# One PSUM tile of six banks in place of several pools, and eight attention columns kept in SBUF

## The chip, the core and the metric

The kernel runs on one core of a Trainium2 chip. The metric is the device time of one execution in microseconds (us); the kernel before takes 2475.04 us, the median of three runs (2474.16 to 2475.89). Five engines run side by side, each taking its own instructions in order: PE (matrix products), PEld (the loading of PE's stationary operand), DVE and ACT (element-wise work), POOL (element-wise work, little used here), and the queues that issue DMAs, of which SP's carries nearly all loads. PE can write its products only into PSUM, a memory of eight banks of 512 float32 values per partition, from which DVE or ACT copies or adds them into SBUF. This copying is called an eviction below.

## The reference

One layer of a decoder that mixes three branches, for a prompt of 1024 tokens and eight sample tokens (TT = 1032 columns in all), width 1024:

```python
xn = rmsnorm(x)
sc_b, sc_c, sc_x, z, xbc, dt_raw, q, gates = split(xn @ w_in)
y_a = (sc_b * conv3(sc_c * sc_x)) @ w_sc_out                  # short convolution
xs, bm, cm = split(silu(conv4(xbc) + b))                      # Mamba-2 SSD, 32 heads x 64, state 128
y_b = group_rmsnorm((ssd(xs, dt, bm, cm) + d * xs) * silu(z)) @ w_ssm_out
y_c = softmax(q @ mem_k.T / 16) @ mem_v @ w_attn_o            # 4 heads x 256, 256 memory tokens
x += (g_a * y_a + g_b * y_b + g_c * y_c) @ w_merge_o          # g = sigmoid(gates)
x += (silu(rmsnorm(x) @ w_gate) * (rmsnorm(x) @ w_up)) @ w_down
y = rmsnorm(x)
```

The sample tokens have key and value caches of their own, so their attention is computed apart from the prompt's. Beside y the new states of the convolutions and of the SSD and the memory's keys and values are returned.

## The kernel before

Activations lie transposed in SBUF: 128 rows of the model width by 1032 columns of tokens, eight such tiles for the width. Every float32 operand of a large product is split into a high and a low part (`split_act` and `st_split`: an ACT copy for the high part, a DVE subtraction for the low one), and a product is three products of these parts.

There are two kinds of large product. A **plain product** (`gemm`, L200) makes one block of 128 output rows by 1032 columns in a buffer of three banks from `mm_ps` (L67): the pool `pmm` has two such buffers, taken in turn, so that one can be evicted while the next is filled. A **Strassen pair** (`strassen`, L311) makes two neighbouring blocks of output rows at once from seven half-size products, in the order B11, T1, nT2, B21, T3, B22, T4. Each has 24 rows of two matmuls (L266) into a buffer of two banks from `st_ps` (L257). There are three such buffers, `m0`, `m1` and `m2`, each a tile of its own, in the pools `pst1` and `pst`: B11, nT2, T3 and T4 go into the first (`pa`), each but B11 added onto what stands there, T1 and B22 into the second (`pb`), B21 into the third (`pc`). After a product its buffer is read at once into the quarter of the result that needs it: B11, T1 and nT2 by ACT (L321), or by DVE where the result is added into x (`into`, L319), B21, T3 and B22 by DVE (L380, L395, L398), and T4 by whoever called. Which of the three buffers plays which part alternates from one Strassen pair to the next (`tags`), with a special order for the first two.

Six banks serve the large products, and the two left (`psm`, L70) the small ones: transposes, scores, the SSD's states. The six are given out by pools that are closed and opened again where the kernel passes from plain products to Strassen pairs or back.

In order of time:

- to about 130 us: x is loaded, normed and transposed; the products dt and B0 (`ps_dt`, `ps_B0`), then C0, z0 and z1 as plain products; the first Strassen pair (Z2).
- 130 to 957: the other 39 Strassen pairs of the input projection (X, Z, G, C, B), with the convolutions on DVE.
- 957 to 1585: the SSD's scan and the attention in small matmuls, among them as plain products the queries (`ps_q`, evicted at L806), four gates (L816), and the 24 output products of the two first branches (`po`, L1440, L1444, L1447).
- 1585 to 1680: the attention's output (`po3`, L1729), eight plain products.
- 1680 to 1770: the merge (`pm`, L1800, evicted at L1807) in halves of 516 columns, in 16 buffers.
- 1770 to 2215: gate and up of the FFN, 22 Strassen pairs. Six of them (`early`) have their products B11 and B21 made ahead in `st_early` (L272) together.
- 2215 to 2473: eight Strassen pairs of the down projection, added into x by DVE; from 2378 on eight plain products (`pd`, L2000) and a last part (`pl`, L2052 to L2062) with three products in one buffer of three banks, each bank evicted by an instruction of its own; the last norm and the stores.

The order on each engine is worked out ahead, when the program is made, from the order in which the kernel states the instructions and from modelled durations. Waits between engines follow from which instructions read and write a tile.

The attention's result for the prompt is written to `at_d` in DRAM by column block, and the eight sample columns, computed into `o_s` (64 columns of the constant tile `tri`), by a DMA of their own in `s_back` (L1610). `out_load` (L1398) loads a tile of `at_d`, all 1032 columns, with one DMA on SP's queue as input of the attention's output product; two of these eight loads are put ahead of it by `out_ahead`.

Of the kernel before, what the change touches and what calls it, by code (L numbers as in the profile page):

```python
# [9 lines left out]
F32 = mybir.dt.float32  # L10
# [4 lines left out]
PSUM = bass.MemoryType.PSUM  # L15
DRAM = bass.MemoryType.DRAM

P = 128
D = 1024
T = 1024  # L20
NS = 8
TT = T + NS
NCH = 3
# [24 lines left out]
def tile_kernel(ctx: ExitStack, tc, a, o):  # L48
    nc = tc.nc
    V, S, G, PE, SY = nc.vector, nc.scalar, nc.gpsimd, nc.tensor, nc.sync  # L50
# [10 lines left out]
    ev = ctx.enter_context(tc.tile_pool(name="ev", bufs=5))  # L61
    dp = ctx.enter_context(tc.tile_pool(name="scratch", bufs=1, space=DRAM))
    psm = ctx.enter_context(tc.tile_pool(name="psm", bufs=2, space=PSUM))
    mm_stack = ExitStack()
    pmm = [mm_stack.enter_context(tc.tile_pool(name="pmm", bufs=2, space=PSUM))]

    def mm_ps(name):  # L67
        return pmm[0].tile([P, NCH, 512], F32, tag="mm", name=name)

    def sm_ps(name):  # L70
        return psm.tile([P, 512], F32, tag="sm", name=name)
# [24 lines left out]
    tri = cp.tile([P, P], F32, tag="tri", name="tri")  # L96
# [87 lines left out]
    def tick():  # L184
        if pend:
            f = pend.popleft()
            if f is not None:
                f()
# [42 lines left out]


    HS = [slice(0, HT), slice(HT, TT)]
    pst = [None]
    freed = [None]
    count = [0]

# [3 lines left out]
    def st_raw(src, name):  # L241
        raw = wp.tile([P, 1024], F32, tag="raw", name=name)
        if len(src.shape) == 4:
            for t in range(2):
                in_turn("raw", SY.dma_start(raw[:, t * 512 : (t + 1) * 512].rearrange("p (k c) -> p k c", k=4), src[:, t]))
            return raw
        in_turn("raw", SY.dma_start(raw.rearrange("p (k c) -> p k c", k=KD), src))
        return raw

    def st_split(src, name, n=1024):  # L250
        hi = wp.tile([P, 1024], F32R, tag="whi", name=name + "h")
        lo = wp.tile([P, 1024], F32R, tag="wlo", name=name + "l")
        in_turn("hi", S.copy(hi[:, :n], src))
        in_turn("lo", V.tensor_sub(lo[:, :n], src, f32(hi)[:, :n]))
        return hi, lo

    def st_ps(tag, name):  # L257
        return pst[0].tile([P, 2, 512], F32, tag=tag, name=name)

    def st_prod(forms, ps, w, off, f, start):  # L260
        for kt in range(4):
# [49 lines left out]
    def strassen(  # L311
        src1, src2, forms, nm, sums, outs, early=None, after_t3=None, ready=None, hook=None, into=False,
        refill=None, following=None,
    ):


        def first(dst, ps):
            if into:
                V.tensor_tensor(dst, ps, dst, op=ALU.add)  # L319
            else:  # L320
                S.copy(dst, ps)  # L321

        def used(f):
            turning.append(refill(f) if refill is not None else None)
            if len(turning) > LATE:
                g = turning.popleft()
                if g is not None:
                    g()


        lead = ahead.pop() if ahead else None
        if lead is not None:
            raw1, raw2 = lead[0], st_raw(src2, f"{nm}r2")
        elif ready is None and early is None:
            raw1, raw2 = st_raw(src1, f"{nm}r1"), st_raw(src2, f"{nm}r2")
        if count[0] == 0:
            tags = ("m2", "m1", "m0")
        elif count[0] == 1:
            tags = ("m1", "m2", "m0")
        else:  # L340
            tags = ("m0", "m1", "m2") if count[0] % 2 == 0 else ("m2", "m1", "m0")
        count[0] += 1
        pa, pb = (st_ps(t, f"{nm}{t}") for t in tags[:2])

        def prod(ps, w, off, f, start):
            st_prod(forms, ps, w, off, f, start)

        o11, o12, o21, o22 = outs()
        if early is None:
            pc = st_ps(tags[2], f"{nm}{tags[2]}")  # L350
            wA = st_split(raw1, f"{nm}A") if lead is None else lead[1]
            prod(pa, wA, 0, "B11", True)
        else:
            tick()
        if ready is not None:
            raw1, raw2, sa, wS, wT = ready
        elif early is not None:
            raw1, raw2, sa, wS = st_sums(src1, src2, nm, sums, freed[0])
        else:
            sa = sums(f"{nm}sa")  # L360
            V.tensor_add(sa[:, :512], raw2[:, :512], raw2[:, 512:])
            V.tensor_add(sa[:, 512:], sa[:, :512], raw1[:, :512])
            wS = st_split(sa, f"{nm}S")
            first(o11, hv(pa))
            used("B11")
        if ready is None:
            sb = st_adds2(raw1, raw2, sa, nm, sums)
        if early is None:
            tick()
        if hook is not None:  # L370
            hook()
        prod(pb, wS, 0, "T1", True)
        first(o22, hv(pb))
        used("T1")
        prod(pa, wS, 512, "nT2", early is not None)
        if early is None:
            first(o12, hv(pa))
            used("nT2")
            prod(pc, wA, 512, "B21", True)
            V.tensor_tensor(o11, hv(pc), o11, op=ALU.add)  # L380
            used("B21")
        else:
            S.copy(o21, o12)
            V.tensor_sub(o22, o22, o12)
            freed[0] = V.tensor_tensor(o12, hv(pa), o12, op=ALU.add).ins
        if ready is None:
            wT = st_split(sb, f"{nm}T")
        if following is not None:
            raw = st_raw(following, f"{nm}f")
            wD = st_split(raw2[:, 512:], f"{nm}D", 512)  # L390
        tick()
        prod(pa, wT, 0, "T3", False)
        if after_t3 is not None:
            after_t3()
        V.tensor_tensor(o22, o22, hv(pa), op=ALU.subtract)  # L395
        used("T3")
        prod(pb, wT, 512, "B22", False)
        V.tensor_tensor(o12, o12, hv(pb), op=ALU.subtract)  # L398
        used("B22")
        tick()  # L400
        if following is None:
            wD = st_split(raw2[:, 512:], f"{nm}D", 512)
        else:
            ahead.append((raw, st_split(raw, f"{nm}F")))
        prod(pa, wD, 0, "T4", False)
        used("T4")
        if into:
            V.tensor_tensor(o21, o21, hv(pa), op=ALU.subtract)
            return
        if early is not None:  # L410
            V.tensor_tensor(o21, hv(pa), o21, op=ALU.add)
            return o21
        return hv(pa)
# [9 lines left out]
    at_d = dram("at_d", [8, P, TT])  # L423
# [17 lines left out]
    qs_d = dram("qs_d", [NS, D])  # L441
    os_d = dram("os_d", [NS, D])

    tail_sc = cp.tile([P, 1, 10, 8], F32, tag="tail_sc", name="tail_sc")
    tail_xc = cp.tile([P, 3, 11, 8], F32, tag="tail_xc", name="tail_xc")
    qs = cp.tile([P, 8, NS], F32, tag="qs", name="qs")
# [11 lines left out]
    h_xc = ch.tile([P, 24, 24], F32, tag="h_xc", name="h_xc")  # L458
    xn = [(act_tile("ah", f"xnh{k}"), act_tile("al", f"xnl{k}")) for k in range(KD)]
    xw = [act_tile(("ah", "al")[k % 2], f"xw{k}", F32) for k in range(KD)]  # L460
    ps_dt, ps_b0 = mm_ps("ps_dt"), mm_ps("ps_B0")

    with tc.tile_pool(name="p0", bufs=1) as p0:
        xin = []
# [12 lines left out]
        for key, src, n in (  # L477
# [14 lines left out]
            while done < n:  # L492
                b, off = divmod(at, P)
# [117 lines left out]
    for src, dst, nr, nt in (  # L611
# [4 lines left out]
        for q0 in range(0, nt, per):  # L616
            t = ev_tile(f"hist{nr}_{q0}", (nr, per * P))
# [710 lines left out]
        for kt in range(4):  # L1328
            split_to(*xforms["T3"][kt], raw3[kt // 2][:, HS[kt % 2]])

    mm_stack.close()
    mm_stack = ExitStack()
    st_stack = ExitStack()
    pst[0] = st_stack.enter_context(tc.tile_pool(name="pst1", bufs=1, space=PSUM))
    for i in (2, 4, 6, 8, 10, 12):
        z_pair(i, plain3 if i == 2 else None)
    flush()
# [38 lines left out]
            split_to(*xforms["T3"][kt], b12s[kt // 2][:, HS[kt % 2]])  # L1376

    gate_pair(18, plain)
    st_stack.close()
    pa_stack.close()  # L1380
    ch_stack.close()
    pmm[0] = mm_stack.enter_context(tc.tile_pool(name="pmm1", bufs=2, space=PSUM))

# [11 lines left out]

    def out_load(src, k):  # L1398
        t = ev_tile(f"in0{k}")
        SY.dma_start(t[:, :TT], src[k])  # L1400
        ahead.append(t)

    def out_in(src):
# [96 lines left out]
    if True:  # L1500
# [1 line left out]
        kTl = at.tile([P, KD, MEM], F32R, tag="kTl", bufs=1, name="kTl")  # L1502
        vh = at.tile([P, 2, D], F32R, tag="vh", bufs=1, name="vh")
        vl = at.tile([P, 2, D], F32R, tag="vl", bufs=1, name="vl")
        o_s = tri[:, :64].rearrange("p (t b) -> p t b", t=8)
        sc_s = tri[:, 64:].rearrange("p (m b h) -> p m b h", m=2, b=NS)
        pTs = qs.rearrange("p t b -> p (t b)").rearrange("p (m c) -> p m c", m=2)

# [94 lines left out]
        def s_back():  # L1603
            t = ev_tile("osr", (NS, D))
            SY.dma_start(t, os_d)
            ps = sm_ps("psob")
            for i in range(8):
                PE.transpose(ps[:, i * NS : (i + 1) * NS], t[:, i * P : (i + 1) * P], ident[:NS, :NS])
            V.tensor_copy(o_s.rearrange("p t b -> p (t b)"), ps[:, :64])
            SY.dma_start(at_d[:, :, T:TT].rearrange("t p b -> p t b"), o_s)  # L1610

        heads = {}
        slot = [None]
# [173 lines left out]
    for half in range(2):  # L1787
        sq = ev_tile(f"sq{half}")
        for m in range(KD):
# [16 lines left out]
            t = x2[m][:, HS[half]]  # L1806
# [12 lines left out]
            flush()  # L1819
            norm_half(1, sq)  # L1820
    aux_stack.close()
    mm_stack.close()

    st_stack = ExitStack()
    pst[0] = st_stack.enter_context(tc.tile_pool(name="pst", bufs=1, space=PSUM))
    pfx = st_stack.enter_context(tc.tile_pool(name="fx", bufs=2))
    fx["T4"] = lambda part, nm: pair_of(pfx.tile([P, AW], F32R, tag=part, name=nm))  # L1830

# [131 lines left out]
                into=True, hook=opening if ch == 0 and m == 0 else None, **turn,  # L1963
            )
    st_stack.close()
    pmm[0] = ctx.enter_context(tc.tile_pool(name="pmm2", bufs=2, space=PSUM))
    fin = ctx.enter_context(tc.tile_pool(name="fin", bufs=1))

    def hidden(j):
# [129 lines left out]
```

## Time and profile before

| | |
|---|---|
| median of three runs | 2475.04 us |
| profiled execution, its own time | 2474.8 us |
| its span (first to last instruction) | 2472.7 us |
| granted TensorE clock, mean | 0.994 |
| PE busy | 2428.5 us (98%) |
| PEld, DVE, ACT, POOL busy | 93%, 64%, 43%, 5% |
| chain that ended last | PE 86%, DMA 5%, DVE 5%, ACT 2% |

By stretch, in us (PE's and DVE's busy time):

| stretch | length | PE | DVE |
|---|---|---|---|
| 0 to 60 | 60 | 50.5 | 38.8 |
| 60 to 130 | 70 | 65.7 | 57.0 |
| 130 to 957, Strassen pairs | 827 | 824.5 | 558.8 |
| 957 to 1585, SSD and attention | 628 | 615.6 | 372.7 |
| 1585 to 1770, attention output and merge | 185 | 183.7 | 106.5 |
| 1770 to 2215, gate and up | 445 | 444.8 | 282.9 |
| 2215 to 2380, down | 165 | 160.3 | 117.4 |
| 2380 to 2473, end | 93 | 83.4 | 50.2 |

A row of the timeline reads: start in us, duration in us, engine, line, operation, the tile written and the tiles read (buffer numbers left out), shape, how many instructions the row joins, and in brackets how long the engine sat idle before it and what ended that. A row joining several matmuls lasts from the first one's start to the last one's end, and since matmuls overlap in PE, rows overlap too. A row of the waits reads: who waited for what, the us in total, how many times, and the longest. In a table by stretch, the stretch and its length come first, then the busy time with the number of instructions in brackets for each engine, then the granted clock, the DMA's busy share and GB/s. In the table of groups the count is followed by the busy time in us and the mean of one in ns, and then by the idle time ahead of them and its enders.

### The profile page before, as it was taken

What the parts mean: (1) busy time and instruction counts of PE and PEld (TensorE: products, weight loads), DVE (VectorE), ACT (ScalarE), POOL (GpSimd) and SP (SyncE); (2) the same over time, 40 slices, a digit from 0 to 9 for tenths busy, and PEclk for the clock granted to TensorE, in tenths of its full rate; (3) what the DMA queues carried; (4) which work ended last, traced back from release to release, by engine and by line L of the source; (5) the groups of instructions that cost most, each with busy time, mean ns of one, the idle gap of its engine ahead of it and who ended that gap; (6) DMA issues with size and microseconds to landing.
All of it is one profiled execution on the core that took longest, in us unless ns stands there. A gap on an engine that the chain in (4) does not pass through costs nothing.

```text
span 2472.7 us, 45688 instructions
## 1 busy us (share of the span) xinstructions
PE 2428.5 (98%) x18946; PEld 2310.5 (93%) x18946; DVE 1584.3 (64%) x2601; ACT 1067.1 (43%) x1712; POOL 114.8 (5%) x163
## 2 busy tenths in 40 slices
PE   8999999999999999999999999999999999999998
PEld 6899999999999999888888888899999999999998
DVE  6844586777677774666767562454787555476755
ACT  6654455354545535556545441223453333342322
POOL 0100000000000000121120000000000000000000
PEclk8999999999999999999999999999999999999999
DMA  6344434344344456667878677874454323264421
GB/s 195 121 139 154 132 102 153 112 130 131 108 137 137 129 154 210 194 207 254 265 219 286 205 265 238 266 241 153 141 174 134 108 86 112 74 231 132 156 85 69
DMA packets 359662, 404.42 MB, mean 164 GB/s; under 512 B 17446, under 2 KB 286870, under 8 KB 359447
## 3 DMA queue, kind: packets, MB, share of 16 engines
q1 hardware_dynamic: 339006, 343.79, 44.6%
q10 hardware_dynamic: 20449, 57.71, 6.0%
q8 instruction: 149, 2.44, 0.4%
q14 instruction: 58, 0.48, 0.1%
HBM read 286.35 MB, written 115.32 MB: 162 GB/s over the span
## 4 chain that ended last, share of the span: by engine, by line
PE 86%; DMA 5%; DVE 5%; ACT 2%; issue 1%; SPq 0%; ACTq 0%; POOL 0%; DVEq 0%
PE po L220 12%; PE ps_q L220 4%; PE pm L1800 3%; PE ps_g L220 2%; PE pd L220 1%; PE py L1041 1%; PE pss L1054 1%; PE po L1033 1%; PE Z2m L266 1%; PE Z4m L266 1%; PE X8m L266 1%; PE d12m L266 1%; PE C2m L266 1%; PE C4m L266 1%; PE G18m L266 1%
## 5 line engine op out<-in xcount | busy, mean ns | idle before, releaser
L986 ACT ACTIVATE r<-r,acum 128x128 f32<-128x128 f32 x256 | 79.2, 392 | 5.1 <-DMA r<-ac_d 4.7
L757 DVE SCALAR_TENSOR_TENSOR ax<-u,prm,ax 128x1024 f32<-128x1024 f32 x44 | 56.3, 1279 | 0.0
L927 ACT ACTIVATE st<-st,es 128x128 f32<-128x128 f32 x128 | 41.5, 392 | 26.4 <-DMA st<-in_state_ssm_dram 23.9
L1018 POOL TENSOR_TENSOR xdd<-xdt,decst 128x512 f32<-128x512 f32 x32 | 37.1, 1160 | 292.2 <-DVE xdt L1014 292.2
L1447 DVE TENSOR_TENSOR yr<-po,yr 128x1032 f32<-128x1032 f32 x8 | 9.8, 1230 | 55.1 <-PE po L220 45.2
L1037 DVE TENSOR_TENSOR y<-po,ea 128x512 f32<-128x512 f32 x28 | 19.3, 690 | 38.9 <-PE po L1033 38.9
L1012 DVE TENSOR_TENSOR r<-r,cbm 128x1024 f32<-128x1024 f32 x32 | 39.2, 1224 | 2.5
L929 DVE SCALAR_TENSOR_TENSOR st<-sr,dts,st 128x128 f32<-128x128 f32 x128 | 40.3, 345 | 0.4
L1011 ACT COPY bT<-bp 128x128 f32<-128x128 f32 x32 | 8.5, 265 | 64.3 <-DVE cbm L1009 64.2
L2034 ACT ACTIVATE fj<-psy 128x512 f32<-128x512 f32 (+1 forms) x18 | 10.7, 596 | 59.1 <-PE psy L2032 59.0
L933 DVE SCALAR_TENSOR_TENSOR sr<-st,sr 128x128 f32<-128x128 f32 x128 | 35.2, 285 | 1.1
L1054 PE MATMUL pss<-xdd,bT 128*128 128x512 f32 x64 | 33.4, 604 | 2.3 <-ACT bT L1011 2.3
L1041 PE MATMUL py<-r,xdt 128*64 128x128 f32 x512 | 35.0, 279 | 0.0
L987 ACT ACTIVATE r<-r 128x1024 f32<-128x1024 f32 x32 | 33.9, 1058 | 0.7
L1014 DVE TENSOR_TENSOR xdt<-xp,dtT 128x512 f32<-128x512 f32 x32 | 21.9, 684 | 18.7 <-PE xp L1007 18.5
L1807 DVE TENSOR_TENSOR x<-pm,xT 128x516 f32<-128x516 f32 x16 | 11.1, 695 | 35.1 <-PE pm L1800 35.1
L1067 POOL TENSOR_TENSOR s<-s,cdec 128x512 f32<-128x512 f32 x28 | 32.1, 1145 | 4.5 <-DVE s L1060 3.9
L1041 PEld LDWEIGHTS py<-r,xdt 128*64 128x64 f32 x512 | 27.3, 136 | 4.2 <-issue 0.5
L1033 PE MATMUL po<-bc,s 128*128 128x128 f32 x224 | 29.6, 275 | 0.0
L760 DVE SCALAR_TENSOR_TENSOR ax<-u,prm,ax 128x1032 f32<-128x1032 f32 x22 | 28.3, 1286 | 0.0
L1178 DVE SCALAR_TENSOR_TENSOR x<-x,prm,sqa 128x1032 f32<-128x1032 f32 x16 | 19.7, 1288 | 13.3 <-ACT sqa L1174 13.3
L1033 PEld LDWEIGHTS po<-bc,s 128*128 128x128 f32 x224 | 27.7, 191 | 0.5
(9066 smaller groups left out, 9044.0 us busy)
## 6 DMA issues: line engine op xcount, KB each, us to landing
r<-ac_d SPq DMA_DIRECT2D x32, 512.0 KB
gt<-gt_d SPq DMA_DIRECT2D x24, 516.0 KB
xs_d<-ax ACTq DMA_DIRECT2D x22, 516.0 KB
gt_d<-G ACTq DMA_DIRECT2D x20, 516.0 KB
x<-xs_d SPq DMA_DIRECT2D x16, 516.0 KB
zs<-zs_d SPq DMA_DIRECT2D x16, 516.0 KB
yb_d<-x SPq DMA_DIRECT2D x16, 516.0 KB
in<-yb_d SPq DMA_DIRECT2D x16, 516.0 KB
```

The lines of the kernel that those rows point to most:

```text
L220: PE.matmul(out[:, c : c + n], wt[:, ks], x[:, c : c + n], start=(k == 0 and i == 0), stop=(k == nk - 1 and i == 2),)
L266: PE.matmul(hv(ps)[:, c : c + n], wt[:, ks], x[:, c : c + n], start=(start and kt == 0 and i == 0), stop=(kt == 3 and i == 2), skip_group_ ...
L757: V.scalar_tensor_tensor(acc[:, :T], u[:, j : j + T], w[j], acc[:, :T], op0=ALU.mult, op1=ALU.add)
L927: S.activation(st[:, i], st[:, i], AF.Copy, scale=es[:, g * 4 + i, b : b + 1])
L929: V.scalar_tensor_tensor(st[:, i], rb, dts[:, g * 4 + i, b : b + 1], st[:, i], op0=ALU.mult, op1=ALU.add)
L986: S.activation(r[:, j, :], r[:, j, :], AF.Relu, scale=-1.0, bias=acum[:, c, h : h + 1])
L1012: V.tensor_tensor(r, r, bc(cbm.unsqueeze(1), [P, HPG, P]), op=ALU.mult)
L1018: G.tensor_tensor(b3(xdd, HPG), b3(xdt, HPG), bc(decst[:, c, hs].unsqueeze(2), [P, HPG, 64]), op=ALU.mult)
L1033: PE.matmul(po[:, t * P : (t + 1) * P], state["s"][:, t * P : (t + 1) * P], bcg[1][:, cs], start=True, stop=True,)
L1041: PE.matmul(py[hp : hp + 64, (h // 2) * P : (h // 2 + 1) * P], xdt[:, h * 64 : (h + 1) * 64], r[:, (h % 2) * 4 + h // 2, :], start=True, s ...
L1054: PE.matmul(pss, bT, xdd, start=True, stop=True)
L1800: PE.matmul(hv(ps)[:, c : c + n], wt[:, ks], x[:, half * HT + c : half * HT + c + n], start=(k == 0 and i == 0), stop=(k == KD - 1 and i = ...
```

## The change

All six banks become one tile, `six`, taken once and kept for the whole kernel. `mm_ps` returns its first or last three banks by turns (`side`), `st_ps` two of the six, so that a buffer is a slice of the tile and no longer a tile of its own. All closing and opening of pools for these banks goes. Strassen pairs alternate their buffers from the first on, without a special order, and each sets `side` so that a plain product after it begins on the banks that T4 does not use. `ps_B0` and `ps_dt` change places.

`out_load` loads only the 1024 prompt columns of `at_d`, and POOL copies the eight sample columns from `o_s` into each of the eight tiles; the DMA that stored them in `at_d` goes, and `o_s` is named earlier.

```diff
--- before.py
+++ after.py
@@ -61,11 +61,14 @@
     ev = ctx.enter_context(tc.tile_pool(name="ev", bufs=5))
     dp = ctx.enter_context(tc.tile_pool(name="scratch", bufs=1, space=DRAM))
     psm = ctx.enter_context(tc.tile_pool(name="psm", bufs=2, space=PSUM))
-    mm_stack = ExitStack()
-    pmm = [mm_stack.enter_context(tc.tile_pool(name="pmm", bufs=2, space=PSUM))]
+    pbig = ctx.enter_context(tc.tile_pool(name="pbig", bufs=1, space=PSUM))
+    six = pbig.tile([P, 2 * NCH, 512], F32, tag="six", name="six")
+    side = [0]
 
     def mm_ps(name):
-        return pmm[0].tile([P, NCH, 512], F32, tag="mm", name=name)
+        i = side[0]
+        side[0] = 1 - i
+        return six[:, NCH * i : NCH * (i + 1)]
 
     def sm_ps(name):
         return psm.tile([P, 512], F32, tag="sm", name=name)
@@ -231,7 +234,6 @@
 
 
     HS = [slice(0, HT), slice(HT, TT)]
-    pst = [None]
     freed = [None]
     count = [0]
 
@@ -255,7 +257,8 @@
         return hi, lo
 
     def st_ps(tag, name):
-        return pst[0].tile([P, 2, 512], F32, tag=tag, name=name)
+        i = int(tag[1:])
+        return six[:, 2 * i : 2 * i + 2]
 
     def st_prod(forms, ps, w, off, f, start):
         for kt in range(4):
@@ -333,12 +336,8 @@
             raw1, raw2 = lead[0], st_raw(src2, f"{nm}r2")
         elif ready is None and early is None:
             raw1, raw2 = st_raw(src1, f"{nm}r1"), st_raw(src2, f"{nm}r2")
-        if count[0] == 0:
-            tags = ("m2", "m1", "m0")
-        elif count[0] == 1:
-            tags = ("m1", "m2", "m0")
-        else:
-            tags = ("m0", "m1", "m2") if count[0] % 2 == 0 else ("m2", "m1", "m0")
+        tags = ("m0", "m1", "m2") if count[0] % 2 == 0 else ("m2", "m1", "m0")
+        side[0] = 1 - count[0] % 2
         count[0] += 1
         pa, pb = (st_ps(t, f"{nm}{t}") for t in tags[:2])
 
@@ -441,6 +440,7 @@
     qs_d = dram("qs_d", [NS, D])
     os_d = dram("os_d", [NS, D])
 
+    o_s = tri[:, :64].rearrange("p (t b) -> p t b", t=8)
     tail_sc = cp.tile([P, 1, 10, 8], F32, tag="tail_sc", name="tail_sc")
     tail_xc = cp.tile([P, 3, 11, 8], F32, tag="tail_xc", name="tail_xc")
     qs = cp.tile([P, 8, NS], F32, tag="qs", name="qs")
@@ -458,7 +458,8 @@
     h_xc = ch.tile([P, 24, 24], F32, tag="h_xc", name="h_xc")
     xn = [(act_tile("ah", f"xnh{k}"), act_tile("al", f"xnl{k}")) for k in range(KD)]
     xw = [act_tile(("ah", "al")[k % 2], f"xw{k}", F32) for k in range(KD)]
-    ps_dt, ps_b0 = mm_ps("ps_dt"), mm_ps("ps_B0")
+    ps_b0, ps_dt = mm_ps("ps_B0"), mm_ps("ps_dt")
+    side[0] = 1
 
     with tc.tile_pool(name="p0", bufs=1) as p0:
         xin = []
@@ -1328,10 +1329,6 @@
         for kt in range(4):
             split_to(*xforms["T3"][kt], raw3[kt // 2][:, HS[kt % 2]])
 
-    mm_stack.close()
-    mm_stack = ExitStack()
-    st_stack = ExitStack()
-    pst[0] = st_stack.enter_context(tc.tile_pool(name="pst1", bufs=1, space=PSUM))
     for i in (2, 4, 6, 8, 10, 12):
         z_pair(i, plain3 if i == 2 else None)
     flush()
@@ -1376,10 +1373,8 @@
             split_to(*xforms["T3"][kt], b12s[kt // 2][:, HS[kt % 2]])
 
     gate_pair(18, plain)
-    st_stack.close()
     pa_stack.close()
     ch_stack.close()
-    pmm[0] = mm_stack.enter_context(tc.tile_pool(name="pmm1", bufs=2, space=PSUM))
 
 
 
@@ -1397,7 +1392,11 @@
 
     def out_load(src, k):
         t = ev_tile(f"in0{k}")
-        SY.dma_start(t[:, :TT], src[k])
+        if src is at_d:
+            SY.dma_start(t[:, :T], src[k, :, :T])
+            G.tensor_copy(t[:, T:TT], o_s[:, k, :])
+        else:
+            SY.dma_start(t[:, :TT], src[k])
         ahead.append(t)
 
     def out_in(src):
@@ -1502,7 +1501,6 @@
         kTl = at.tile([P, KD, MEM], F32R, tag="kTl", bufs=1, name="kTl")
         vh = at.tile([P, 2, D], F32R, tag="vh", bufs=1, name="vh")
         vl = at.tile([P, 2, D], F32R, tag="vl", bufs=1, name="vl")
-        o_s = tri[:, :64].rearrange("p (t b) -> p t b", t=8)
         sc_s = tri[:, 64:].rearrange("p (m b h) -> p m b h", m=2, b=NS)
         pTs = qs.rearrange("p t b -> p (t b)").rearrange("p (m c) -> p m c", m=2)
 
@@ -1607,7 +1605,6 @@
             for i in range(8):
                 PE.transpose(ps[:, i * NS : (i + 1) * NS], t[:, i * P : (i + 1) * P], ident[:NS, :NS])
             V.tensor_copy(o_s.rearrange("p t b -> p (t b)"), ps[:, :64])
-            SY.dma_start(at_d[:, :, T:TT].rearrange("t p b -> p t b"), o_s)
 
         heads = {}
         slot = [None]
@@ -1819,13 +1816,11 @@
             flush()
             norm_half(1, sq)
     aux_stack.close()
-    mm_stack.close()
 
 
 
 
     st_stack = ExitStack()
-    pst[0] = st_stack.enter_context(tc.tile_pool(name="pst", bufs=1, space=PSUM))
     pfx = st_stack.enter_context(tc.tile_pool(name="fx", bufs=2))
     fx["T4"] = lambda part, nm: pair_of(pfx.tile([P, AW], F32R, tag=part, name=nm))
 
@@ -1963,7 +1958,6 @@
                 into=True, hook=opening if ch == 0 and m == 0 else None, **turn,
             )
     st_stack.close()
-    pmm[0] = ctx.enter_context(tc.tile_pool(name="pmm2", bufs=2, space=PSUM))
     fin = ctx.enter_context(tc.tile_pool(name="fin", bufs=1))
 
     def hidden(j):
```

## The prediction

> **What bounds the kernel now.** I read the busy table first, then the busy time by stretch, then the waits of TensorE, then the timeline at the places where a PSUM buffer changes hands.
>
> ```profile
> PE 2428.5 (98%) x18946; PEld 2310.5 (93%) x18946; DVE 1584.3 (64%) x2601; ACT 1067.1 (43%) x1712; POOL 114.8 (5%) x163
> PE 86%; DMA 5%; DVE 5%; ACT 2%; issue 1%; SPq 0%; ACTq 0%; POOL 0%; DVEq 0%
> ```
> ```profile
> 130.00:957.00 827.00, 824.46 (x6926) 822.99 (x6926) 558.77 (x1032) 389.39 (x560) 32.62 (x82) 1.00 0.44 134
> ```
>
> PE is busy 98% of the span and makes 86% of the chain that ended last. In the long stretch of Strassen pairs it is idle 2.5 us of 827 (PE's busy time is the first column after the length), at a granted clock of 1.00. So every eviction of PSUM now happens while PE fills another buffer. Whatever ends that overlap adds its price once per eviction; whatever only trims the remaining waits is worth a few us.
>
> **The question that decides.** Before, each buffer is a tile of its own; after, all six banks are one tile and a buffer is a slice of it. Does the program then still know that an eviction of one slice and a matmul into another don't concern each other? One place of the old kernel already uses one tile so: the last stage makes three products in three banks of one tile `pl` and evicts each bank with an instruction of its own (L2062).
>
> ```profile
> 2415.87 0.34 PE L2060 MATMUL pl<-h21h,wl0l 128*128 128x384 f32 x1
> 2416.39 0.34 PE L2060 MATMUL pl<-h21h,wl0l 128*128 128x384 f32 x1
> 2416.92 0.34 PE L2060 MATMUL pl<-h21h,wl1l 128*128 128x384 f32 x1
> 2417.29 1.02 DVE L2062 TENSOR_TENSOR x<-pl,x 128x384 f32<-128x384 f32 x2 [3.46 <-PE pl L2060]
> ```
>
> These are the last matmuls of the three banks. Bank 0 is complete at 2415.87 + 0.34 = 2416.21, bank 1 at 2416.73, bank 2 at 2417.26. DVE has been idle for 3.46 us, and still begins with bank 0 only at 2417.29, just after bank 2. DVE was free, its data was ready for 1.1 us, so the order is kept for the whole tile, not for the bank. Rows show this in one direction, a read waiting for writes of other banks. That a write waits for reads of other banks is my inference: a record that knows no banks can't know them for one direction only.
>
> With that, the new tile means: every eviction waits for all matmuls written ahead of it, every matmul into the six banks waits for all evictions written ahead of it. Changing sides no longer overlaps anything: PE stands still during each eviction.
>
> **The price of one stop.** Two present seams show it, where PE already has to wait for a DVE and an ACT eviction.
>
> ```profile
> 2376.93 0.40 PE L266 MATMUL d16m<-h1T41l,d16Dh 128*128 128x256 f32 x2
> 2377.16 0.40 PE L266 MATMUL d16m<-h1T41h,d16Dl 128*128 128x256 f32 x2
> 2377.60 0.69 DVE L408 TENSOR_TENSOR x<-x,d16m 128x516 f32<-128x516 f32 x1 [1.26 <-PE d16m L266]
> 2378.44 0.71 PE L220 MATMUL pd<-h16h,wd160h 128*128 128x512 f32 x3 [0.87 <-DVE x L408]
> ...
> 97.66 1.03 ACT L858 ACTIVATE z<-ps_z 128x1032 f32<-128x1032 f32 x1
> 98.74 0.50 PE L266 MATMUL Z2m<-xnh,Z2Ah 128*128 128x256 f32 x2 [1.60 <-ACT z L858]
> ```
>
> Undisturbed, matmul rows begin 0.24 apart (2376.93 and 2377.16, to the rounding), though each lasts 0.40. At the DVE seam the next begins 2378.44 - 2377.16 = 1.28 later, so it loses 1.04: 0.16 of lost overlap, 0.04 until DVE begins, 0.69 of eviction, 0.15 until PE begins. The ACT eviction ends at 98.69 and PE begins at 98.74; with the same 0.04 before it, its price is the eviction plus 0.16 + 0.04 + 0.05 = 0.25. So: ACT d + 0.25, DVE d + 0.35.
>
> **How many stops.** Over the whole span, first the ACT evictions of L321, then those of L398, of which each Strassen has one by DVE, then the DVE form of the first three, L319 (all in the last third).
>
> ```profile
> 0.00:2473.00 2473.00, 102.30 (x174) 0.99 0.51 164
> ```
> ```profile
> 0.00:2473.00 2473.00, 48.09 (x70) 0.99 0.51 164
> ```
> ```profile
> 1680.00:2473.00 793.00, 16.50 (x24) 1.00 0.39 129
> ```
>
> There are 70 Strassens. 56 evict B11, T1 and nT2 by ACT (0.59, so 3 x 0.84 = 2.52), B21, T3 and B22 by DVE (0.69, so 3 x 1.04 = 3.12), and T4 by one or the other (0.85 to 1.04, taken 0.9): 6.5 each, 364. Eight add into x by DVE alone (L319 x24): 7 x 1.04 = 7.3 each, 58. Six have their B11 and B21 made earlier and five evictions left: 0.84 + 4 x 1.04 = 5.0 each, 30, and the 12 early copies by ACT 12 x 0.84 = 10. Strassens together: **+462**. One took 20.00 us before, the row being of the chain of waits:
>
> ```profile
> 937.34 20.00 PE G18m L266 x168
> ```
>
> The plain products, by groups (count, then total and mean in ns):
>
> ```profile
> L806 ACT COPY q<-ps_q 128x1032 f32<-128x1032 f32 x8 | 8.1, 1007 | 0.0
> L816 ACT ACTIVATE g<-ps_g 128x1032 f32<-128x1032 f32 x4 | 4.1, 1032 | 0.8 <-PE ps_g L220 0.8
> L1440 DVE TENSOR_TENSOR gt<-po,gt 128x1032 f32<-128x1032 f32 x8 | 9.8, 1228 | 2.4 <-PE po L220 2.3
> L1444 ACT COPY yr<-po 128x1032 f32<-128x1032 f32 x8 | 8.2, 1023 | 0.0
> L1447 DVE TENSOR_TENSOR yr<-po,yr 128x1032 f32<-128x1032 f32 x8 | 9.8, 1230 | 55.1 <-PE po L220 45.2 <-DMA out_p_xconv_dram<-cs 10.0
> L1729 DVE TENSOR_TENSOR gt<-po,gt 128x1032 f32<-128x1032 f32 x8 | 9.9, 1232 | 28.3 <-PE po L220 27.4 <-DMA gt<-gt_d 0.7
> L1807 DVE TENSOR_TENSOR x<-pm,xT 128x516 f32<-128x516 f32 x16 | 11.1, 695 | 35.1 <-PE pm L1800 35.1
> L2000 DVE TENSOR_TENSOR x<-pd,x 128x1032 f32<-128x1032 f32 x8 | 9.9, 1233 | 18.3 <-PE pd L220 18.3
> L2062 DVE TENSOR_TENSOR x<-pl,x 128x384 f32<-128x384 f32 x16 | 8.1, 550 | 10.2 <-PE pl L2060 10.2
> ```
>
> The first five stand beside SSD and attention, whose matmuls use the two other banks and can be put into a stop: 8 x 1.26 + 4 x 1.28 + 8 x 1.58 + 8 x 1.27 + 8 x 1.58 = 51; none hidden gives 51, all hidden 0, I take half, 25. L1729, L1807 and L2000 have no such work: 8 x 1.58 + 16 x 1.04 + 8 x 1.58 = 42. Three products at the head add 4. `pl` is 12 tiles whose evictions take 8.1 us in the wide form and, in two narrower forms, I estimate some 5 more: 13 + 12 x 0.35 = 17. Together **+88**. Four seams stand still already and are not paid twice (below): **-4**.
>
> **Queues.** A stop also lasts while the evicting engine finishes something else.
>
> ```profile
> 604.49 0.41 PE L266 MATMUL B2m<-nT22ah,B2Sl 128*128 128x256 f32 x2
> 604.73 0.62 ACT L253 CAST B2Dh<-B2r 128x512 fp32r<-128x512 f32 x1 [2.07 <-PE B2m L266]
> 605.26 0.59 ACT L321 COPY b<-B2m 128x516 f32<-128x516 f32 x1
> ```
>
> This product ends at 604.90 and its copy starts 0.36 later, behind a cast; the DVE eviction at the seam above started 0.04 late. Over some 570 stops, nothing gives 0, 0.4 each 228. DVE and ACT will be less busy per us than now (64% and 43% over a longer span), so nearer the lower end: 0.15, **+86**.
>
> Sum: 462 + 88 - 4 + 86 = **+632** on the profiled 2474.8, which is 0.2 below the median: **3107 us**.
>
> **The other edits.** They are small under either answer. The order of `ps_B0` and `ps_dt` and of the first two Strassens' banks only chooses which eviction is waited for; with one tile all are. The eight sample columns by POOL instead of by DRAM remove one store (L1610, one issue on SP's queue ahead of the first `at_d` load) and add eight copies of 128x8, for which the nearest rows run from 0.2 us to one of 8.27:
>
> ```profile
> 82.41 8.27 POOL L830 COPY bcs<-aC 128x8 f32<-128x8 f32 x1 [8.21 <-ACT aC L826]
> 341.42 0.19 POOL L830 COPY bcs<-ax 128x8 f32<-128x8 f32 x1 [2.44 <-ACT ax L826]
> ```
>
> POOL has nothing else there, and each copy runs beside the 4 KB-per-partition load of the same buffer: 0, and at the worst, the first load waited for 8.27, +8. I take 0.
>
> **Rivals.** *The tile is ordered by bank after all* (or only reads wait), so it does what it says. Against it: the `pl` rows. For it: nothing in them shows a write that waits. Then only present waits shrink:
>
> ```profile
> PE Z2m L266 <- ACT z L858: 1.6, 1, 1.6
> PE g0e L266 <- ACT g2Eh L253: 0.9, 1, 0.9
> PE pd L220 <- DVE x L408: 0.9, 1, 0.9
> PE po L220 <- ACT b00h L178: 0.9, 1, 0.9
> PE po L220 <- DVE b00l L179: 0.5, 1, 0.5
> ```
>
> These are the seams where pools closed and opened, and the attention's last product, whose inputs wait for the store and loads of `at_d`. Sum 4.8; Z2's second product waits for its own weights too, for which I leave 0.5: 2474.8 - 4.3, **2470.5**, not slower. It decides as soon as the first matmul of T1 starts while B11's copy runs. The Trainium skill ("Perfetto Trace Analysis", Optimizing Tensor Performance, Matmuls) speaks for it: it says that independent groups of matmuls should rotate through different banks so that evicting one overlaps the next group. By that rule the change is worth the -4.3; the trace agrees for separate tiles, but for banks of one tile the `pl` rows disagree.
>
> *The stops also cost clock.* After the one long idle time of PE its rows begin 0.86 apart (61.45, 62.31), and then 0.54 (62.85):
>
> ```profile
> 58.73 1.20 PE L220 MATMUL ps_C<-xnh,wC0h 128*128 128x512 f32 x3 [4.25 <-ACT uB L837]
> ...
> 61.45 1.06 PE L220 MATMUL ps_C<-xnh,wC0h 128*128 128x512 f32 x3
> 62.31 0.70 PE L220 MATMUL ps_C<-xnl,wC0h 128*128 128x512 f32 x3
> 62.85 0.64 PE L220 MATMUL ps_C<-xnh,wC0l 128*128 128x512 f32 x3
> ```
>
> Half speed for 1 us after each of 570 stops adds 285: **3390**. Against it: idle times here are about 1 us, and after the 1.60 before Z2m the seam above has no such run of slow rows. The Trainium skill ("TensorE: Matmul & The Clock Gate", A second HAM failure mode: psum-queue depth-cycling) tells of a kernel where short idles between groups made the clock oscillate; no run here shows it yet.
>
> **How the numbers follow.** Forecast 0.82, ordered by bank 0.15, clock 0.03. Evictions alone, with no latencies, no queue and the SSD's stops hidden, are 186 x 0.59 + 248 x 0.69 + 56 x 0.62 for the Strassens plus 35 + 13 for the rest: +364, 2840. Queues of 0.4 and nothing hidden: 462 + 88 + 26 - 4 + 228 = +800, 3275. That range, 2840 to 3275, leaves the two rivals out, 0.18. No change means within 0.2%, 5 us, about what a measurement of this kernel can tell: the first rival's -4.3 lies at that edge, so faster 0.08, same 0.06, slower 0.86.
>
> **What would show it.** In the changed profile PE's busy share falls to about 80%, a Strassen of 20.0 us takes 27, and PE's waits list evictions (L321, L380, L395, L398) hundreds of times at about 0.6 to 0.9 us. Wrong would be: T1's matmuls beginning beside L321, PE at 98%, the only differences at the four seams. The size is wrong if stops are much longer than 1.04 (queues) or matmul rows are further apart than 0.24 between stops (clock).

## The result: 28% slower

The changed kernel takes 3161.03 us (median of four runs, 3156.59 to 3166.97), the kernel before 2475.47 us in the same comparison. The ratio is 1.2769 with a 95% interval of 1.2743 to 1.2796, or +686 us. The profiled execution has a span of 3155.8 us, 683 more than before.

The page of the profile after, its table of busy time:

```profile
PE 2597.0 (82%) x18946; PEld 2370.9 (75%) x18946; DVE 1605.9 (51%) x2601; ACT 1075.4 (34%) x1714; POOL 123.3 (4%) x171
```

The work is the same: as many matmuls, and DVE and ACT are busy as long as before (1606 against 1584 us, 1075 against 1067). PE's share has gone from 98% to 82%. The waits of PE after, as who waited for what, us in total, times, longest:

```profile
PE six L269 <- ACT u L324: 27.4, 33, 1.6
PE six L269 <- ACT G L324: 27.1, 30, 1.5
PE six L269 <- DVE x L322: 23.1, 23, 2.0
...
PE six L269 <- DVE G L394: 10.8, 10, 1.8
PE six L269 <- DVE G L379: 10.6, 10, 1.4
```

L324 is the old L321, L322 the old L319, L379, L394 and L397 the old L380, L395 and L398: PE waits for the evictions, each time it has filled a buffer. The timeline after shows two such stops in one Strassen pair:

```profile
702.07 0.41 PE L269 MATMUL six<-nT22ah,C2Sl 128*128 128x256 f32 x2
702.27 0.62 ACT L255 CAST C2Dh<-C2r 128x512 fp32r<-128x512 f32 x1 [2.96 <-PE six L269]
702.79 0.58 ACT L324 COPY c<-six 128x516 f32<-128x516 f32 x1
...
703.42 0.30 PEld L269 LDWEIGHTS six<-xnh,C2Ah 128*128 128x128 f32 x2 [1.16 <-ACT c L324]
703.43 0.51 PE L269 MATMUL six<-xnh,C2Ah 128*128 128x256 f32 x2 [0.95 <-ACT c L324]
...
703.65 0.31 PEld L269 LDWEIGHTS six<-xnl,C2Ah 128*128 128x128 f32 x2
703.77 0.41 PE L269 MATMUL six<-xnl,C2Ah 128*128 128x256 f32 x2
...
704.01 0.40 PE L269 MATMUL six<-xnh,C2Al 128*128 128x256 f32 x2
...
706.15 0.40 PE L269 MATMUL six<-xnh,C2Al 128*128 128x256 f32 x2
...
706.66 0.69 DVE L379 TENSOR_TENSOR c<-six,c 128x516 f32<-128x516 f32 x1 [3.05 <-PE six L269]
...
707.41 0.51 PE L269 MATMUL six<-xnh,C2Th 128*128 128x256 f32 x2 [0.86 <-DVE c L379]
```

L379 reads the buffer of B21 (`pc`); the matmul at 707.41 begins T3 in another one (`pa`), which had been read at 702.79 already. Its weights lay ready (their split had ended at 692.4) and its banks were free. It starts 0.06 after DVE has ended with the other banks. So a write waits for a read of other banks of the same tile, the direction that the rows of before did not show.

Where the time went, by the first matmul of each stretch in both timelines (the last column is what the prediction's terms give for the stretch, without its 86 us for queues and its -4 for the seams, which it did not divide; the stretch of the down projection begins with T1 of its first pair, whose B11 is made at the end of gate and up):

| stretch | before | after | difference | predicted |
|---|---|---|---|---|
| head and first pair | 126.2 | 140.6 | +14.4 | 10 |
| 39 pairs of the input projection | 831.8 | 1109.4 | +277.5 | 253 |
| SSD, attention, `po` | 624.5 | 678.7 | +54.2 | 25 |
| `po3` | 92.3 | 108.4 | +16.1 | 13 |
| `pm` and the early products | 131.3 | 161.3 | +30.1 | 27 |
| gate and up, 22 pairs | 408.4 | 592.2 | +183.9 | 134 |
| down, 8 pairs | 164.0 | 229.3 | +65.3 | 58 |
| `pd` | 33.9 | 46.8 | +12.8 | 13 |
| `pl` and the end | 60.3 | 89.1 | +28.8 | 17 |

### The profile page after: what moved, and what is told of

The parts are those of the page before. It is cut to its first block, busy times and chain, and to the rows that moved or that the text cites. A ratio compares the mean times of both kernels' runs of the same rounds, so it can differ in the third digit from the quotient of the medians.

```text
span 3155.8 us, 45677 instructions
## 1 busy us (share of the span) xinstructions
PE 2597.0 (82%) x18946; PEld 2370.9 (75%) x18946; DVE 1605.9 (51%) x2601; ACT 1075.4 (34%) x1714; POOL 123.3 (4%) x171
## 5 line engine op out<-in xcount | busy, mean ns | idle before, releaser
L322 DVE TENSOR_TENSOR x<-six,x 128x516 f32<-128x516 f32 x24 | 16.7, 694 | 43.6 <-PE six L269 43.5
L1804 DVE TENSOR_TENSOR x<-six,xT 128x516 f32<-128x516 f32 x16 | 11.1, 695 | 50.4 <-PE six L1797 48.1
L324 ACT COPY u<-six 128x516 f32<-128x516 f32 x33 | 19.4, 587 | 48.7 <-PE six L269 42.6
L988 ACT ACTIVATE r<-r 128x1024 f32<-128x1024 f32 x32 | 33.9, 1059 | 0.7
L1446 DVE TENSOR_TENSOR yr<-six,yr 128x1032 f32<-128x1032 f32 x8 | 9.8, 1231 | 47.5 <-PE six L223 47.5
L1055 PE MATMUL pss<-xdd,bT 128*128 128x512 f32 x64 | 33.9, 612 | 0.0
L1726 DVE TENSOR_TENSOR gt<-six,gt 128x1032 f32<-128x1032 f32 x8 | 9.9, 1232 | 45.5 <-PE six L223 45.5
L2056 DVE TENSOR_TENSOR x<-six,x 128x384 f32<-128x384 f32 (+2 forms) x32 | 11.9, 420 | 37.3 <-PE six L2054 37.2
```

The costliest lines, as they stand in the source:

```text
L988: S.activation(r, r, AF.Exp, scale=-1.0)
L1055: PE.matmul(pss, bT, xdd, start=True, stop=True)
```

## The experiments

Theory: the program keeps the order of reads and writes for each tile as a whole, so with one tile PE stands still for every eviction. First rival: one of the change's other parts, or having one tile over the whole kernel, costs the time. Second: the stop is latency or queueing and the eviction itself counts for little. Each experiment starts from the kernel before unless it says otherwise.

**The sample columns alone.** The pools stay; `out_load` and `s_back` are as in the change.

```diff
+    o_s = tri[:, :64].rearrange("p (t b) -> p t b", t=8)
...
-        SY.dma_start(t[:, :TT], src[k])
+        if src is at_d:
+            SY.dma_start(t[:, :T], src[k, :, :T])
+            G.tensor_copy(t[:, T:TT], o_s[:, k, :])
+        else:
+            SY.dma_start(t[:, :TT], src[k])
...
-        o_s = tri[:, :64].rearrange("p (t b) -> p t b", t=8)
...
-            SY.dma_start(at_d[:, :, T:TT].rearrange("t p b -> p t b"), o_s)
```

> The old pools and tiles; only the attention's eight sample columns stay in SBUF. Theory (order kept per tile explains the whole loss): no part of the 686 us is here, 2471 to 2476 us; at best the waits of the attention's output product for its inputs (0.9 + 0.5 us before) shrink. Rival (the copies by POOL are slow, as one of 8.27 us was): +3 to +8 us, and that product waits for POOL.

Measured: 2475.52 us against 2475.46, ratio 0.9996 (0.9987 to 1.0005). The profile of this kernel still shows a small effect: of PE's waits for that product's inputs only one is left. POOL's eight copies take 0.19 to 1.24 us each (three of them 3.52 us from the first one's start to the last one's end), and one cast on ACT waits 0.4 us for them.

```profile
PE po L220 <- ACT b02h L178: 0.4, 1, 0.4
```
```profile
1584.99 3.52 POOL L1403 COPY in<-tri 128x8 f32<-128x8 f32 x3 [4.00 <-DVE yr L1453]
```

So this part is worth at most a few us, less than can be told from no change, and the loss is not in it.

**One tile for the Strassen buffers only.** Opened and closed where the old pools were (the first stretch's `six1` is opened in the same way):

```diff
-        return pst[0].tile([P, 2, 512], F32, tag=tag, name=name)
+        i = int(tag[1:])
+        return pst[0][:, 2 * i : 2 * i + 2]
...
-    pst[0] = st_stack.enter_context(tc.tile_pool(name="pst", bufs=1, space=PSUM))
+    pst[0] = st_stack.enter_context(tc.tile_pool(name="pst", bufs=1, space=PSUM)).tile(
+        [P, 6, 512], F32, tag="six", name="six2"
+    )
```

> The kernel before, but the three Strassen buffers are slices of one tile in each of the two Strassen stretches; plain products keep their two tiles. Theory: the stretches of Strassen pairs lose what they lost in the changed kernel (11 + 278 + 28 + 184 + 65 = 565 us), the others nothing: 3040 us (3015 to 3065), PE at 1.00 of the clock at the end. Rival (the loss comes from keeping one tile over the whole kernel): near 2475 us.

Measured: 3033.36 us, ratio 1.2248 (1.2233 to 1.2264), +558, inside the range.

**One tile for the plain products only.** Two sides of a tile, by turns, in each of the three old pools:

```diff
+    def two_sides(pool):
+        return pool.tile([P, 2 * NCH, 512], F32, tag="mm", name="sides")
...
-        return pmm[0].tile([P, NCH, 512], F32, tag="mm", name=name)
+        i = side[0]
+        side[0] = 1 - i
+        return pmm[0][:, NCH * i : NCH * (i + 1)]
...
```

> The kernel before, but the two buffers of the plain products are the two sides of one tile; Strassen buffers stay three tiles. Theory: the plain stretches lose what they lost in the changed kernel (3 + 54 + 16 + 3 + 13 + 29 = 118 us): 2593 us (2570 to 2605). If the low clock at the changed kernel's end (0.50 over the last 40 us) comes from the stops there, it shows here too; if it comes from the long stretch of stops before, it doesn't, and the end loses some 10 us less. Rival as for the pairs: 2475 us.

Measured: 2602.93 us, ratio 1.0504 (1.0489 to 1.0519), +127, inside the range. The two parts and the columns add up: 558 + 127 + 0 = 685 of 686. So keeping the tile over the whole kernel, the closing of the pools and the order of the first buffers, none of which was run alone, have together no part that can be told from the 7 us of the interval to either side.

This kernel also shows what the low clock at the changed kernel's end goes with. By stretch, the end after, then the end of the kernel with one tile for the plain products, then that with one tile for the pairs, then that of the kernel before (length, PE's busy time, granted clock, DMA share, GB/s):

```profile
3067.00:3108.00 41.00, 35.22 (x187) 0.96 0.10 39
3108.00:3156.00 48.00, 37.28 (x173) 0.53 0.14 56
```
```profile
2560.00:2602.00 42.00, 31.32 (x141) 0.52 0.15 59
```
```profile
2973.00:3003.00 30.00, 29.86 (x182) 1.00 0.13 53
3003.00:3033.30 30.30, 21.07 (x179) 0.95 0.23 89
```
```profile
2433.00:2473.00 40.00, 30.38 (x236) 0.95 0.26 105
```

The clock falls to about half in the last 40 us where the plain products of the end have stops. Where only the pairs have them it ends at 0.95, like the kernel before, though a stretch of 1100 us with stops went before. PE's busy share of these last 40 us doesn't tell the kernels apart (75 to 78% at half clock, 76% before). What it is in the last stretch that lowers the clock is not settled.

**Two of three buffers in one tile.** m0 and m1 are slices of one tile, m2 has its own:

```diff
-        return pst[0].tile([P, 2, 512], F32, tag=tag, name=name)
+        if tag == "m2":
+            return pst[0][0].tile([P, 2, 512], F32, tag=tag, name=name)
+        i = int(tag[1:])
+        return pst[0][1][:, 2 * i : 2 * i + 2]
+
+    def st_open(pool):
+        return pool, pool.tile([P, 4, 512], F32, tag="four", name="four")
...
```

> The kernel before, but of the three Strassen buffers m0 and m1 are slices of one tile and m2 stays a tile of its own. Theory (order per tile, so a stop arises only where an eviction from a tile is followed at once by a product into the same tile): a Strassen pair that begins in m0 has four stops (after B11, T1, T3 and B22), about 1.13 + 1.13 + 1.18 + 1.40 = 4.8 us, one that begins in m2 has none, since its neighbours in time lie in different tiles. So pairs take 20.0 and 24.8 us by turns, 31 x 4.8 plus some 17 for the early ones: +168, 2643 us (2615 to 2670). Rival A (every eviction from a shared tile costs a stop): two thirds of the about 565 us that the Strassen pairs lost, 2850 us. Rival B (slices of one tile are kept apart, and the loss has another cause): 2475 us.

Measured: 2562.19 us, ratio 1.0343 (1.0329 to 1.0356), +87: half of what the theory gave, outside its range, and far from either rival. The pairs don't take 20.0 and 24.8 us by turns either. The timeline of this kernel shows why, at the first stop of a pair that begins in m0 (`four` is the shared tile, `G8m` the pair's m2):

```profile
660.36 0.40 PE L272 MATMUL four<-xnh,G8Al 128*128 128x256 f32 x2
...
660.60 0.40 PE L272 MATMUL G8m<-xnh,G8Ah 128*128 128x256 f32 x2
...
660.80 0.59 ACT L327 COPY G<-four 128x516 f32<-128x516 f32 x1 [0.90 <-PE four L272]
660.84 0.40 PE L272 MATMUL G8m<-xnl,G8Ah 128*128 128x256 f32 x2
...
661.08 0.39 PE L272 MATMUL G8m<-xnh,G8Al 128*128 128x256 f32 x2
...
661.44 0.50 PE L272 MATMUL four<-T10ah,G8Sh 128*128 128x256 f32 x2
```

While ACT empties B11's buffer, PE makes three rows of B21, a product that comes third after this one in the code but lies in the other tile, and goes back to T1 at 661.44. The order on PE is planned, and the plan fills this stop with a product in another tile that is ready; 660.60 to 661.44 holds three rows of 0.24 and loses 0.12, and the row behind 661.44 starts at 661.78, 0.10 late: 0.22 in all, not 1.1. Later in the pair it takes rows of the next pair's B11. So the theory's rule for which evictions cause a stop holds (the write to `four` waits for the read of `four`, the write to `G8m` does not), and my sum was wrong in taking every stop at full price. In the changed kernel no large product lies in another tile, so only the small products, in the two other banks, can fill a stop. With one of the three buffers left out of the shared tile, the pairs' loss falls from 558 to 87 us.

**Every copy by ACT twice**, in the changed kernel and in the one before:

```diff
                 S.copy(dst, ps)
+                S.copy(dst, ps)
```

> The changed kernel, but each of the 174 copies of B11, T1 and nT2 by ACT (0.59 us) is made twice over, the second with the same result. Theory (PE stands still while a product is evicted): each second copy lengthens its stop by its own 0.59 and some 0.03 to start it, 174 x 0.62 = +108 on the changed kernel's 3161: 3269 us (3255 to 3285). Rival (the stop is latency or queue, and the eviction's own length counts for little): 3161 to 3180 us.

> The kernel before with the same 174 copies made twice. Theory (with a tile per buffer the eviction runs beside the next product, and ACT is busy 43%): hidden, 2475 us (2472 to 2481). Rival (ACT's time is near the path already): up to +108, 2583 us.

Measured: the changed kernel so altered takes 3286.36 us, ratio to the kernel before 1.3278 (1.3255 to 1.3302); less the change's own 1.2769 that is +126 us, 0.72 per copy, just above the range that I had given. The second rival (3161 to 3180) falls: a stop grows by about the length of what reads the buffer. By stretch, in the profiled execution (119 us over that of the changed kernel), it is +31 for the 54 copies of the FFN, 0.58 each, as the theory has it, but +89 for the 117 of the input projection, 0.76 each. Four stops in the pairs G make most of the difference. Here is one, and the clock behind it:

```profile
503.55 0.80 PE L269 MATMUL six<-xnh,G2Ah 128*128 128x256 f32 x2 [6.00 <-ACT G L325]
```
```profile
502.30:509.10 6.80, 5.54 (x24) 0.50 0.44 116
```

The four last 5.4 to 6.0 us. At this one ACT's order has updates of the SSD's state (L929) ahead of the copy, and they begin only at 500.45, after ACT has stood idle for 6.07 us until DVE (L931) had done its part. At each of the four the granted clock is 0.50 for 6.8 us.

The kernel before so altered takes 2515.2 us, ratio 1.0159 (1.0144 to 1.0174), +39 where I had forecast none, outside the range. By stretch: +1 in gate and up, +36 in the input projection. There the copies are hidden, but the casts of weights behind them on ACT are not. The waits of PE in this kernel:

```profile
PE G4m L266 <- DVE G4Tl L254: 4.1, 1, 4.1
PE G8m L266 <- DVE G8Tl L254: 2.9, 1, 2.9
```

T3's weights come 2 to 4 us late in seven of the ten pairs G, 18 us in all: ACT casts the high part, DVE takes the low part from it, and the second copies push the casts back. So ACT's 43% is an average, and in these pairs it has little to spare. The clock adds to it. Behind each of the seven waits it is 0.50 for 3.4 to 6.8 us, here after the one of 4.1:

```profile
518.00:524.00 6.00, 4.60 (x21) 0.50 0.49 125
```

That is some 27 us at half speed, so by estimate 14 us more, and the two together are 32 of the 36 us.

**A tile for each bank of `pl`.** This tests the row on which the prediction's sign rested:

```diff
+    mm_stack.close()
+    pone = ctx.enter_context(tc.tile_pool(name="pone", bufs=6, space=PSUM))
...
-            ps = mm_ps(f"pl{n3}{m0}")
+            ps = [pone.tile([P, 512], F32, tag="one", name=f"pl{n3}{m}") for m in ms]
...
```

> The kernel before, but each of the three products of the last stage (pl) has a tile of one bank of its own instead of a third of one tile. Theory (order is kept per tile): the first bank's eviction starts right after its own last matmul, about 1.05 us ahead of the third's end, the second 0.5 ahead, where before all started after the third. DVE isn't the bound there, so the time stays: 2475 us (2472 to 2478; the pool that closes ahead of it can cost one wait of 1.2). Rival (DVE waited for something else): the evictions still start after the third bank's last matmul.

Measured: 2476.24 us against 2476.39, ratio 1.0003 (0.9993 to 1.0012). The timeline of this kernel at the first three products:

```profile
2421.82 0.34 PE L2063 MATMUL pl<-h21h,wl0l 128*128 128x384 f32 x1
...
2422.19 1.60 DVE L2065 TENSOR_TENSOR x<-pl,x 128x384 f32<-128x384 f32 x3 [4.02 <-PE pl L2063]
2422.34 0.34 PE L2063 MATMUL pl<-h21h,wl0l 128*128 128x384 f32 x1
...
2422.86 0.34 PE L2063 MATMUL pl<-h21h,wl1l 128*128 128x384 f32 x1
```

Bank 0's last matmul ends at 2422.16 and its eviction starts at 2422.19, 1.01 us ahead of bank 2's end at 2423.20. Before, it started 0.03 after bank 2's end. Beside the tiles only the pool that gives them out was changed, which can hold up the start of a product but not a read behind it, so what held DVE was the shared tile. Since DVE is not the bound there, it gains nothing.

None of these kernels is faster than the one before by more than can be told.

## Why the prediction was right, and where its sum was off

**The sign and the cause** came out as forecast. The question that the prediction put first, whether the program knows slices of one tile apart, was answered by the `pl` rows in one direction and by inference in the other; the stop at 707.41 and the experiment with one tile for the pairs show the inferred one. The rival "ordered by bank" is refuted by both. The signs that the prediction named came too: PE is busy 82%, and a pair of 20 us takes 28.0 on average over the 34 pairs from X17 on. By the rule of the Trainium skill ("Perfetto Trace Analysis", Optimizing Tensor Performance, Matmuls), independent groups of matmuls should rotate through different banks, so that the eviction of one overlaps the next group's matmuls. The trace differs: the groups rotate and PE waits 0.86 us for the eviction of another bank, because the banks are one tile.

**The number of stops** was right: taking for each eviction the last matmul row into `six` ahead of it and the first one behind it, the timeline after holds 572 stops; the prediction counted "some 570".

**The price of a stop** was 632 / 573 = 1.10 with its queue term, and the whole came out 51 us too low (683 against 632 on the spans). In the stops of the timeline after, outside the SSD's stretch, the mean time from PE's end to the eviction's start is 0.22, where the prediction had 0.04 + 0.15 = 0.19; so the queue term was nearly right as a mean. It is not spread evenly. In the input projection the mean wait before L397 is 0.04, in gate and up 0.66, since there DVE has the next pair's sums ahead of it in 17 of 22 stops. Gate and up lost 184 where the terms without queue gave 134; of these 50 us the waits before L397 make 14, the other queues 23, more than half of them on ACT, and the slow starts of the next paragraph 14. The stop at 702.79 shows the other common queue: a cast of the next weights becomes possible just before the product ends (702.27, and the last row ends at 702.48), and ACT takes it first.

**The term that was left out** is the start after a stop. Rows begin 0.24 apart, but the second row after a stop begins 0.34 after the first (703.43 and 703.77), and the first lasts 0.51 and not 0.40. The median over the 489 stops that a row of a Strassen pair follows is 0.34, and what goes beyond 0.24 adds up to 48 us. The seam that the prediction used for its price has it too (the row after 98.74 lies at 99.09), but I measured the price to the first row behind the stop only. The prediction had named rows further apart than 0.24 as a sign of a lower clock; here they come at a granted clock of 1.00. The weight load for the row behind the stop begins with that row (703.42 and 703.43), that for the next one 0.12 ahead (703.65 and 703.77); whether this is the cause is not shown.

**The pairs that lost little.** That these 48 us come near the 51 that were missing is partly luck, since other terms were off by tens of us both ways. The five pairs Z4 to Z12 lost 11.6 us together (from 126.2 to 273.1 before, from 140.6 to 299.1 after), where 6.5 each makes 33. The prediction let small matmuls fill stops beside the SSD only; here the products of the memory's keys and values (`ps_kv`) do it, as between B11 and T1 of Z4:

```profile
143.22 0.40 PE L269 MATMUL six<-xnh,Z4Al 128*128 128x256 f32 x2
143.46 0.39 PE L1311 MATMUL ps_kv<-wkv01l,memh 128*128 128x256 f32 x2
143.66 0.59 ACT L324 COPY Z<-six 128x516 f32<-128x516 f32 x1 [3.20 <-PE six L269]
...
145.62 0.28 PE L1311 MATMUL ps_kv<-wkv01l,memh 128*128 128x256 f32 x1
145.73 0.41 PE L269 MATMUL six<-T10ah,Z4Sh 128*128 128x256 f32 x2
```

The 34 pairs behind them lost 266 us, 7.8 each, where the prediction has 6.5 and seven times 0.15 for queues, 7.6.

**SSD and attention** were mis-sized: half of 51 us was taken as hidden behind small matmuls, and the stretch lost 54. The 36 stops there last longer than elsewhere, because ACT and DVE have their own work: by the same count L1443 (the old L1444) starts 2.3 us after its product's end on average (twice 7.7, else 0.5 to 0.8), L817 (the old L816) 1.8, of which 1.28 is an ACT_TABLE_LOAD just ahead of it. Together they come to about 89 us and not 51, and the small matmuls fill some 35 of them: it was the length of the stops that was wrong more than the share that is hidden.

**The clock** was a rival for all stops at 3390 us. It did not come about in the long stretches (the granted clock is 1.00 in the input projection at 80% busy), only in the last 48 us at 0.53; there the loss was 29 where 17 was predicted. So at the length that most stops have, about 1 us, it costs nothing; the kernels with every copy twice show it at work behind waits of 2 us and more. The cost of the rest of the change was put at 0, and the run with the columns alone agrees (0.9996).

## What to carry over

Before merging buffers into one allocation, find a place in the present trace where two independent users of one allocation meet, and look whether the second waits for the first: here three rows of a side stage told the sign of a change to the whole kernel. A slice is not a buffer when the order is kept for the tile: double buffering needs two tiles, and one tile left out of three already gave back most of the loss. When costing a stop, measure to the second instruction behind it, not the first.

## What was not expected of the hardware

After a stop of about 1 us PE's second row of two matmuls begins 0.34 us after the first instead of 0.24, at a granted clock of 1.00. Stops of about 1 us leave the clock at 1.00 for 1100 us in one stage, while in the kernels with every copy twice each wait of 2.0 to 6.0 us in the pairs G is followed or met by 3.4 to 6.8 us at 0.50. Where the limit lies is not shown: in the changed kernel's gate and up a wait of 2.22 us (before 2719.0) leaves the clock at 1.00 and one of 2.09 (before 2760.8) doesn't. And a clock of 0.52 to 0.53 goes with stops in the last 40 us, in both kernels that have them there. No run here separates the causes of any of these.
